# A two-layer hybrid trunk on one core: attention values in alternating column halves, recurrence products and low-rank gates over 64 rows in alternating row halves

## The chip, the cores and the metric

The kernel runs on one NeuronCore of a Trainium2 chip. A core has a matrix engine (TensorE, PE in the profile, with its weight loads listed apart as PEld), a vector engine (VectorE, DVE), an engine for activation functions (ScalarE, ACT), a general engine (GpSimd, POOL) and an engine that here only issues transfers (SyncE, SP). Matmul results land in PSUM, which the program divides into eight banks of 128 partitions by 512 float32; the other engines read them from there. Each engine works through its own instruction list strictly in the order in which the list was built, and waits at semaphores for the others.

The metric is device time in microseconds (us) of one launch. Three runs of the kernel before gave 1375.79, 1385.37 and 1380.54 us; their median, 1380.54 us, is the time to compare with.

## What is computed

The input is 1024 tokens of 1024 features. Layer 0 has two head groups beside each other, an RWKV-7 recurrence of 8 heads of width 64 and a sparse attention of 8 heads of width 64 over one shared key and value per token, of which each query keeps 256. Layer 1 is a gated linear attention. Each layer ends in an output projection and a layer norm. The parts that matter here, cut from the reference:

```python
def rwkv7_mix(r, k, v, wd, ad, w0, w2, a0, a2, ...):
    w_log = -jax.nn.softplus(-(w0 + jnp.tanh(wd) @ w2)) - 0.5     # low-rank gate, rank 64
    decay = jnp.exp(-jnp.exp(w_log))
    a = jax.nn.sigmoid(a0 + ad @ a2)                              # low-rank gate, rank 64
    ...
    def step(S, inp):
        r_t, w_t, k_t, v_t, kk_t, b_t = inp
        sa = jnp.einsum('bhvk,bhk->bhv', S, -kk_t)
        S = S * w_t[:, :, None, :] + sa[..., None] * b_t[:, :, None, :] + v_t[..., None] * k_t[:, :, None, :]
        return S, jnp.einsum('bhvk,bhk->bhv', S, r_t)

def dsa_mix(...):   # per block of 128 queries
        s = jnp.where(valid[:, :, None, :], s, -1e30)
        p = jax.nn.softmax(s, axis=-1)
        return jnp.einsum('bqhk,bqkd->bqhd', p, v_sel)

        y = jnp.concatenate([ya, yb], -1).astype(h.dtype) @ e_w_out[j]
```

## The kernel before

The kernel is one program of four stages. First come the input projections, the index scores, the RWKV operands (norms, decays, low-rank gates) and the search for the top-256 threshold; this takes about the first 515 us. From 515 to about 800 us runs the stage that most of the change is in: attention over the selected keys, with the RWKV recurrence in chunks of 64 tokens woven into it. Then follow layer 0's output projection and norm, and last layer 1.

**The order.** The program is written in Python; a scheduler then orders each engine's list by its own idea of when things are ready. Within the attention stage the Python code weaves the two parts by a credit in microseconds: `att(us)` lets the attention generator run until the credit is used, between the steps of the recurrence. The scheduler may move an instruction ahead of others on its engine where no dependence forbids it. What is finally in the list is fixed; an instruction that has to wait holds up all that stand behind it on the engine.

**Attention.** Queries go in 8 tiles of 128. For tile `i` the function `att_logits` makes the logits of all heads (L774, L775, bank `s`), and `att_out` the output: for each key tile `kt` up to `i`, it transposes the probabilities of four heads at a time (L811, bank `st`), once for the even heads (`s` = 0) and once for the odd (`s` = 1), copies them out as `pT[s]` (L813), and multiplies by the values in `values` (L795). The weights are a 128x64 tile of `v_tm`. Bank `po` holds the even heads in partitions 0 to 63 and the odd heads in 64 to 127, so that a matmul of `s` = 0 uses the array's columns 0 to 63 and one of `s` = 1 the columns 64 to 127. Each call of `values` makes four matmuls: two halves of 256 moving columns, each for both `s`. There are 36 calls in all (1 + 2 + ... + 8 key tiles), which is 144 matmuls.

**Recurrence.** The 16 chunks go in 8 units of two. For each chunk, `load_chunk` brings the operand `AT` (the chunk's a and r) into a fresh buffer: for each parity `s`, head by head, its 64 rows hold the data, and the other parity's 64 rows are set to zero by a memset on POOL (L917). `products` (L933) multiplies `BK` (the chunk's b and k of all heads, 128 rows) with `AT`: four matmuls of 128x128 by 128x128 per parity, eight per chunk, each over all 128 rows, of which 64 are zeros. Both parities use PSUM bank `g` in turn. From it ACT copies the part `MAB` (L935), and DVE writes k's products with a into `AT`'s zeroed rows (L936) and those with r into `W` (L937). `increments` (L942) transposes `BD` into bank `x`; `substitute` inverts small triangles on POOL (L964, L965), and `offdiag` finishes the inverse in four steps, all through bank `x` (L990, L999, L1009, L1018). `chain` is the serial part: per chunk Z (L1035), U (L1051), then outputs and new state (L1046, L1058), where the state's decayed part `SP` comes from POOL (L1042). `finish` transposes the normed outputs (L1102, bank `x`).

**Output projection.** When attention is over, its buffers are given to the projection's weights: 16 blocks are loaded (L124), split by ACT (`whi`, L128) and POOL (`wlo`, L129), and used by L728 to L730.

**Gates.** `decays` makes both low-rank gates for a group of heads and half the tokens: two matmuls with 64 rows each (L520), one on rows 0 to 63, the other on 64 to 127, into two banks `ix`. It is called 8 times in the first stage.

## Time and profile before

| | |
|---|---|
| runs | 1375.79, 1385.37, 1380.54 us |
| profiled execution, first to last instruction (span; its own time is given in no other form) | 1379.4 us |
| mean granted TensorE clock | 0.949 of full |
| TensorE busy | 1243.3 us, 90% |
| VectorE busy | 847.8 us, 61% |
| ScalarE busy | 564.0 us, 41% |
| GpSimd busy | 421.1 us, 31% |

A busy share is the time in which at least one instruction of the engine was under way. [...] A float32 matmul leaves two records, one for each of its two passes through the array; transposes and the matmuls of the split float32r operands leave one. Some records are missing.

### The profile page before, as it was taken

The page shows a single profiled execution, that of the slowest core. Times are in us where ns is not written, and L with a number is a line of the kernel's source. Part 1 is how long each engine was busy: PE and PEld are TensorE (multiplying, and loading weights), DVE is VectorE, ACT ScalarE, POOL GpSimd, SP SyncE. Part 2 cuts the span into 40 slices and gives each one's busy share as a digit, 9 for nine tenths or more (in the row PEclk, how much of TensorE's full clock was granted, in tenths as well). Part 3 has the DMA queues.
Part 4 walks back from the last instruction along what each step waited for, and adds up shares of the span by engine and source line. Part 5 has one row for each costly group of instructions (what it writes and reads, how often), then busy time and mean ns, then how long its engine had stood idle before and what let it go on. Part 6 is the DMA issues. An engine that isn't in the chain of part 4 may idle for free. (4 is left out here: it accounts for less than half of the span.)

```text
span 1379.4 us, 21874 instructions
## 1 busy us (share of the span) xinstructions
PE 1243.3 (90%) x8141; PEld 963.6 (70%) x8141; DVE 847.8 (61%) x2029; ACT 564.0 (41%) x1089; POOL 421.1 (31%) x532
## 2 busy tenths in 40 slices
PE   7997797887788988999999879899999999998996
PEld 6976585565566666677766658777578878887885
DVE  5345879999999456768767646683330114453665
ACT  5345757637532425555554432132551123333100
POOL 3313431341424351444444351153112221131122
PEclk9998798998899989999999989999899999999998
DMA  6102311431424378334433376561102220013131
GB/s 206 31 1 76 107 39 31 124 104 50 127 54 122 108 199 216 90 73 120 125 94 78 88 222 214 197 200 60 35 0 61 62 62 0 1 62 103 62 118 62
DMA packets 164634, 130.50 MB, mean 95 GB/s; under 512 B 61424, under 2 KB 138272, under 8 KB 164528
## 3 DMA queue, kind: packets, MB, share of 16 engines
q1 hardware_dynamic: 161728, 122.72, 30.9%
q10 hardware_dynamic: 2800, 6.39, 1.5%
q8 instruction: 64, 1.05, 0.3%
q14 instruction: 42, 0.34, 0.1%
HBM read 86.08 MB, written 42.99 MB: 94 GB/s over the span
## 5 line engine op out<-in xcount | busy, mean ns | idle before, releaser
L129 POOL TENSOR_TENSOR wlo<-wraw,whi 128x512 fp32r<-128x512 f32 (+1 forms) x80 | 100.7, 1275 | 191.2 <-ACT whi L128 126.5
L143 PE MATMUL dn<-xh,chi 128*128 128x512 f32 x336 | 137.6, 410 | 16.6 <-DVE sh L472 8.7
L145 PE MATMUL dn<-xh,clo 128*128 128x512 f32 x336 | 137.3, 409 | 0.0
L144 PE MATMUL dn<-xl,chi 128*128 128x512 f32 x336 | 136.8, 407 | 0.0
L128 ACT CAST whi<-wraw 128x512 fp32r<-128x512 f32 (+1 forms) x80 | 48.6, 613 | 130.9 <-PE dn L144 65.6
L143 PEld LDWEIGHTS dn<-xh,chi 128*128 128x128 f32 x336 | 65.8, 196 | 36.3 <-issue 11.3
L744 POOL TENSOR_TENSOR z<-z,ln 128x1024 f32<-128x1024 f32 x16 | 38.7, 2419 | 166.6 <-DVE z L743 83.2
L144 PEld LDWEIGHTS dn<-xl,chi 128*128 128x128 f32 x336 | 65.9, 196 | 20.9 <-issue 7.4
L145 PEld LDWEIGHTS dn<-xh,clo 128*128 128x128 f32 x336 | 65.8, 196 | 18.6 <-issue 5.0
L153 POOL CAST chi<-craw 128x1024 fp32r<-128x1024 f32 x21 | 25.8, 1231 | 133.3 <-PE dn L144 95.3
L380 DVE SCALAR_TENSOR_TENSOR sc<-rl,wi_s,sc 128x384 f32<-128x384 f32 (+5 forms) x42 | 50.6, 1205 | 24.4 <-ACT rl L375 22.4
L728 PE MATMUL s<-whi,yh 128*128 128x512 f32 x128 | 52.6, 412 | 14.0 <-DVE gny L118 7.1
L795 PE MATMUL po<-pT,v_tm 128*64 128x256 f32 x288 | 62.7, 400 | 0.0
L785 ACT ACTIVATE p<-p,am 128x128 f32<-128x128 f32 (+7 forms) x64 | 49.1, 769 | 18.6 <-DVE am L783 18.1
L154 POOL TENSOR_TENSOR clo<-craw,chi 128x1024 fp32r<-128x1024 f32 x21 | 54.5, 2595 | 0.9
L776 DVE CUSTOM_DVE_ANT_0 p<-s,bias_s 128x512 f32<-128x512 f32 (+1 forms) x80 | 45.4, 591 | 14.8 <-PE s L775 11.9
L729 PE MATMUL s<-wlo,yh 128*128 128x512 f32 x128 | 52.2, 408 | 0.3 <-POOL wlo L129 0.3
L641 DVE TENSOR_SCALAR_CACHE_REDUCE junk<-klo,Lc 128x384 bf16<-128x384 int16 (+1 forms) x64 | 51.8, 809 | 0.6
L641 DVE TENSOR_SCALAR_CACHE_REDUCE junk<-khi,Hc 128x384 bf16<-128x384 int16 (+1 forms) x64 | 51.8, 809 | 0.5
L1354 POOL TENSOR_TENSOR vg<-vg,sg 128x512 f32<-128x512 f32 x16 | 20.5, 1285 | 103.2 <-DVE vg L1399 66.8
L165 PE MATMUL gt<-whi,hh 128*128 128x512 f32 x128 | 51.9, 406 | 0.0
L730 PE MATMUL s<-whi,yl 128*128 128x512 f32 x128 | 51.5, 402 | 0.0
(470 smaller groups left out, 3429.1 us busy)
## 6 DMA issues: line engine op xcount, KB each, us to landing
wraw<-in_o_w_in_dram SPq DMA_DIRECT2D x48, 256.0 KB
craw<-in_e_w_in_dram SPq DMA_DIRECT2D x21, 512.0 KB
xt<-in_x_dram SPq DMA_DIRECT2D x8, 512.0 KB
d_q<-qiT SPq DMA_DIRECT2D x8, 512.0 KB
d_ar<-ar SPq DMA_DIRECT2D x8, 512.0 KB
d_gate<-sg SPq DMA_DIRECT2D x8, 512.0 KB
qT<-d_q SPq DMA_DIRECT2D x8, 512.0 KB
BK<-d_bk SPq DMA_DIRECT2D x8, 512.0 KB
```

The lines of the kernel that those rows point to most:

```text
L129: sub.tensor_sub(lo, raw, f32(hi))
L143: PE.matmul(pst, wh[:, cs], ah[:, k, sl], start=(k == 0), stop=False)
L144: PE.matmul(pst, wh[:, cs], al[:, k, sl], start=False, stop=False)
L145: PE.matmul(pst, wl[:, cs], ah[:, k, sl], start=False, stop=(k == NK - 1))
L154: G.tensor_sub(lo, raw, f32(hi))
L165: PE.matmul(pst, ah[:, k, sl], wh, start=(k == 0), stop=False)
L380: E.scalar_tensor_tensor(acc[:, a:b], r, w, acc[:, a:b], op0=ALU.mult, op1=ALU.add)
L641: V.tensor_scalar(junk[:, :n], x, c[:, z:z + 1], None, op0=ALU.is_ge, op1=ALU.add, accum_out=cnt[:, z:z + 1])
L728: PE.matmul(pt, yh[:, k, :], wh, start=(k == 0), stop=False)
L729: PE.matmul(pt, yh[:, k, :], wl, start=False, stop=False)
L730: PE.matmul(pt, yl[:, k, :], wh, start=False, stop=(k == NK - 1))
L795: inorder(PE.matmul(po[RS[s], c:c + PVN], v_tm[:, kt, :], pT[s][:, c:c + PVN], start=(kt == 0 and c == 0), stop=(kt == i), skip_group_chec ...
```

## The change

Three groups of matmuls are rewritten, with a helper `after` that gives the scheduler an order to keep between two instructions (no semaphore, and other instructions may still come between).

1. `values`: for each half of the columns now `s` = 1 first, then `s` = 0, and all four matmuls are chained in this order.
2. `products`: each matmul takes only its parity's 64 rows of `BK` and `AT`. The two parities alternate, chained, and go into two PSUM banks, `g` and `x`. The zeroed rows are no longer read here. `AT` becomes six fixed buffers in turn instead of a pool; only the r half of the zero rows, which `chain` still reads, is cleared, once per buffer ahead of the loop, and the memset per chunk and parity goes.
3. `decays`: the two gate matmuls are issued before either activation, chained.

All other differences are dropped comments and docstrings.

```diff
+    def after(prev, ins):
+        if prev is not None:
+            tc.add_manual_dep(ins.ins, prev.ins.name, mybir.DependencyInfo(
+                mybir.DependencyClass.NoSync, mybir.DependencyReason.DATA), reason="side by side")
+        return ins
...
     def decays(j, h, pool):
-        for th, row, bc in ((thw, 0, HW0), (tha, CH, HA0)):
-            pt = ptile("ix")
-            PE.matmul(pt, w2a2[row:row + CH, j * P:(j + 1) * P], wa[row:row + CH, sl], start=True, stop=True)
+        pts, last = [ptile("ix"), ptile("ix")], None
+        for pt, row in zip(pts, (0, CH)):
+            last = after(last, PE.matmul(pt, w2a2[row:row + CH, j * P:(j + 1) * P], wa[row:row + CH, sl],
+                                         start=True, stop=True))
+        for th, pt, bc in zip((thw, tha), pts, (HW0, HA0)):
             A.activation(th, pt, AF.Tanh, scale=0.5, bias=drv[:, bc + j:bc + j + 1])
...
         def values(kt, pT):
+            last = None
             for c in range(0, 512, PVN):
-                for s in range(2):
-                    inorder(PE.matmul(po[RS[s], c:c + PVN], v_tm[:, kt, :], pT[s][:, c:c + PVN],
-                                      start=(kt == 0 and c == 0), stop=(kt == i), skip_group_check=True))
+                for s in (1, 0):
+                    last = after(last, PE.matmul(po[RS[s], c:c + PVN], v_tm[:, kt, :], pT[s][:, c:c + PVN],
+                                                 start=(kt == 0 and c == 0), stop=(kt == i), skip_group_check=True))
...
+    ATB = []
+    for z in range(6):
+        ATB.append(rt([P, 4, 2, P], f"AT{z}"))
+        for s in range(2):
+            G.memset(ATB[z][RS[1 - s], :, s, CH:], 0.0)
+
     def load_chunk(u, cc):
-        S = rt([P, 4, 2, P], "AT", 6)
+        S = ATB[c % 6]
         for s in range(2):
-            G.memset(S[RS[1 - s], :, s, :], 0.0)
             nc.sync.dma_start(S[RS[s], :, s, :], d_ar[RS[s], :, c, :])
...
     def products(u, cc):
+        pts, last = [ptile("g"), ptile("x")], None
+        for j in range(4):
+            for s in range(2):
+                last = after(last, PE.matmul(pts[s][:, j * P:(j + 1) * P], BK[RS[s], j * 2 + cc, :], AT[RS[s], j, s, :],
+                                             start=True, stop=True))
         for s in range(2):
             b_, k2_ = RS[s], RS[1 - s]
-            pt = ptile("g")
-            for j in range(4):
-                inorder(PE.matmul(pt[:, j * P:(j + 1) * P], BK[:, j * 2 + cc, :], AT[:, j, s, :], start=True, stop=True))
-            p3 = pt.rearrange("p (j t) -> p j t", t=P)
+            p3 = pts[s].rearrange("p (j t) -> p j t", t=P)
             A.copy(MABv[b_, :, cc, :], p3[b_, :, 0:CH])
```

Since the scheduler orders the lists anew, the places that matter are shown as they stand in the two programs. A row has the line of the kernel, the operation, its output and inputs, the output's shape and how many follow each other. The lines of the changed kernel lie 9 to 19 higher. The first place is on TensorE, one key tile of attention; `po` is the values' bank, `st` the transposes' and `s` the logits'. Before:

```order
L811 MATMUL st<-ident,p 128x128 x4
L795 MATMUL po<-pT,v_tm 64x256
L774 MATMUL s<-KH_93,qT 128x512
L775 MATMUL s<-KL,qT 128x512
L774 MATMUL s<-KH_93,qT 128x128
L775 MATMUL s<-KL,qT 128x128
L811 MATMUL st<-ident,p 128x128 x4
L795 MATMUL po<-pT,v_tm 64x256 x3
```

The same work in the changed program:

```order
L822 MATMUL st<-ident,p 128x128 x4
L784 MATMUL s<-KH_93,qT 128x512
L785 MATMUL s<-KL,qT 128x512
L784 MATMUL s<-KH_93,qT 128x128
L785 MATMUL s<-KL,qT 128x128
L822 MATMUL st<-ident,p 128x128 x4
L806 MATMUL po<-pT,v_tm 64x256 x4
```

Before, one matmul of `s` = 0 stood alone and three (`s` = 1, 0, 1) stood together, at all 36 key tiles (at one of them the three are split further); now four stand together, at 34 of the 36, and two and two at the other two.

The second place is on TensorE too, the products of one chunk (`g` and `x` written from `BK`). Before:

```order
L1035 MATMUL zu<-RUV,AT 64x64 x8
L942 MATMUL x<-ident,BD 128x128
L933 MATMUL g<-AT,BK 128x128 x4
L1046 MATMUL sy<-RUV,AT 64x64 x8
L942 MATMUL x<-ident,BD 128x128 x3
L811 MATMUL st<-ident,p 128x128 x4
```

And in the changed program:

```order
L949 MATMUL g<-AT_3793,BK 128x128
L1077 MATMUL sy<-RUV,W 64x64 x9
L961 MATMUL x<-ident,BD 128x128 x4
L1077 MATMUL sy<-RUV,W 64x64 x7
L822 MATMUL st<-ident,p 128x128 x4
L784 MATMUL s<-KH_93,qT 128x512
L785 MATMUL s<-KL,qT 128x512
L784 MATMUL s<-KH_93,qT 128x256
L785 MATMUL s<-KL,qT 128x256
L949 MATMUL x<-AT_3793,BK 128x128
L949 MATMUL g<-AT_3793,BK 128x128
L949 MATMUL x<-AT_3793,BK 128x128
```

Before, each parity's four products stood together, in 32 groups of four. Now the first product of `g` stands alone and, after other work, the remaining seven alternate between `x` and `g`; it is so at all 16 chunks.

The third place is on POOL at the end of the stage, where the last decayed states `SP` and the split of the projection's weights (`wlo`) meet. Before:

```order
L965 TENSOR_TENSOR Xt<-Xt,itmp 128x8
L1042 TENSOR_TENSOR SP<-RUV,PC 64x256 x2
L972 TENSOR_TENSOR TT<-td,own 128x512
L1042 TENSOR_TENSOR SP<-RUV,PC 64x256 x2
L129 TENSOR_TENSOR wlo<-wraw,whi 128x512 x16
```

And in the changed program:

```order
L984 TENSOR_TENSOR Xt<-Xt,itmp 128x8
L136 TENSOR_TENSOR wlo<-wraw,whi 128x512 x2
L991 TENSOR_TENSOR TT<-td,own 128x512
L136 TENSOR_TENSOR wlo<-wraw,whi 128x512 x2
L1061 TENSOR_TENSOR SP<-RUV,PC 64x256 x2
L136 TENSOR_TENSOR wlo<-wraw,whi 128x512 x12
L1061 TENSOR_TENSOR SP<-RUV,PC 64x256 x2
```

Attention now ends two chunks earlier in the recurrence, so that the last two `SP` stand among the weights' splits and no longer ahead of them. On TensorE, 95 matmuls of the projection now stand ahead of the last chunk's first one (L1054), where none stood before. The two gate matmuls keep their places: in both programs the same 8 to 24 rows of other work stand between the two of a call.

## The prediction, made before the changed kernel ran

> **What bounds the kernel now.** I first asked which engine fills the stage of the change: the table by stretches, here attention with the recurrence (515 to 781 us), its tail until the projection's weights are in (781 to 819), and what follows. After the bounds of the stretch come busy time and instructions of PE, PEld, DVE, ACT and POOL, then the granted clock.
>
> ```profile
> 515.00:781.00 266.00, 248.84 (x3739) 186.97 (x3738) 190.68 (x566) 141.37 (x341) 111.84 (x316) 0.98 0.45 110
> 781.00:819.00 38.00, 24.06 (x247) 17.93 (x246) 19.37 (x41) 18.19 (x36) 20.10 (x16) 0.82 0.74 215
> 819.00:1000.00 181.00, 170.82 (x718) 128.21 (x719) 99.55 (x206) 52.98 (x79) 44.44 (x28) 0.95 0.44 142
> ```
>
> In the first stretch TensorE is idle for 17.2 us of 266, and VectorE, next, is busy for 72%. TensorE bounds this stage, at full clock, so that work taken off it there should shorten the run. In the tail it is idle for 13.9 us of 38. Next, its waits in the stage (us in total, times, longest):
>
> ```profile
> PE x L990 <- DVE Tn L985: 6.3, 4, 2.5
> PE x L942 <- DMA BD<-d_bd: 3.0, 1, 3.0
> PE g L933 <- issue: 1.4, 1, 1.4
> ...
> PE g L933 <- POOL AT L917: 0.3, 1, 0.3
> ```
>
> None repeats often; no single releaser sets the pace. Last, what a matmul really costs: the timeline of one key tile (start, duration until the last of a group ends, records), with two close-ups of the run of six records.
>
> ```profile
> 563.22 0.65 PE L795 MATMUL po<-pT,v_tm 128*64 128x256 f32 x2
> 563.80 0.50 PE L774 MATMUL s<-KH,qT 128*128 128x512 f32 x1
> ...
> 564.89 0.27 PE L811 MATMUL st<-ident,p 128*128 128x128 f32 x1
> 565.10 1.08 PE L795 MATMUL po<-pT,v_tm 128*64 128x256 f32 x6
> 566.10 0.50 PE L774 MATMUL s<-KH,qT 128*128 128x512 f32 x1
> ...
> 565.10 0.44 PE L795 MATMUL po<-pT,v_tm 128*64 128x256 f32 x2
> ...
> 565.58 0.38 PE L795 MATMUL po<-pT,v_tm 128*64 128x256 f32 x1
> ...
> 565.79 0.38 PE L795 MATMUL po<-pT,v_tm 128*64 128x256 f32 x1
> ```
>
> Two records at 565.10 are over within 0.44 us: the first passes of two matmuls in different column halves run side by side. The pair has its two passes done by 565.58. The third matmul then has the array alone: its passes start at 565.58 and 565.79, 0.21 apart. So a pair costs what one matmul costs. A change between array shapes (128x128, 128x64, 32x32) adds about 0.15: 0.10 of emptying before the start (564.89 plus a pass of 0.11 is 565.00, the next starts at 565.10) and 0.05 in the first pass (565.10 to 565.58 is 0.48, where two later passes take 0.43).
>
> **The change part by part.**
>
> *Values.* The lone matmul of each key tile joins the three and rides beside the one that had no partner. 36 key tiles save two passes of 0.215 each, 0.43: 15.5 us, all on the path while TensorE is the bound.
>
> [...]
>
> ```profile
> 565.09 0.20 PEld L795 LDWEIGHTS po<-pT,v_tm 128*64 128x64 f32 x4 [0.17 <-issue]
> ...
> L795 PEld LDWEIGHTS po<-pT,v_tm x288: 132/136/227, 515.4 to 780.8; 128*64 128x64 f32 x144
> ```
>
> *Products.* A group of four costs eight passes one after the other, of 0.108 each: 128 columns, half of the 256 that took 0.215. The last starts at 640.83, and with one more pass and a change of shape the next instruction at 641.04.
>
> ```profile
> 639.95 1.16 PE L933 MATMUL g<-AT,BK 128*128 128x128 f32 x8
> ...
> 640.83 0.28 PE L933 MATMUL g<-AT,BK 128*128 128x128 f32 x1
> 641.04 0.28 PE L1051 MATMUL zu<-Zs,TT 128*64 128x64 f32 x2
> ...
> 641.53 0.37 ACT L935 COPY MAB<-g 64x256 f32<-64x256 f32 x1
> ...
> 643.99 0.41 DVE L936 TENSOR_TENSOR AT<-g,GM 64x256 f32<-64x256 f32 x1
> 644.33 0.40 DVE L937 TENSOR_TENSOR W<-g,GM 128x256 f32<-128x256 f32 x1
> ```
>
> A chunk now has 16 passes (two groups). With 64 rows each the parities use different row halves. If these run side by side as the column halves do, the lone product costs two passes and the seven cost as much as the four of one row half, eight: 10 in place of 16. That saves 6 x 0.108 x 16 chunks = 10.4 us. The trace shows no matmuls in two row halves with the same columns, so that this has ends: 0, if they follow each other, and 10.4. I take 10.4, since the nearest rows, the pair in column halves above and the 32x32 products below (46 records within 0.58 us, each in another row and column quarter than the one before), both overlap. [...]
>
> ```profile
> 775.36 0.58 PE L990 MATMUL x<-Tn,MAB 32*32 32x16 f32 x46
> ```
>
> *Changes of shape.* 64x128 is a shape of its own, next to none of its neighbours. Counted over both orders from the first values to the last recurrence product, without the projection's matmuls, there are 271 changes before and 251 now: the values' merged groups save more than the split products add. 20 x 0.15 = 3.0 us less.
>
> *Gates.* One gate matmul has two passes of 512 columns, 0.43 each (twice the values' 0.215; with a change of shape, the 1.06 below from 238.19 to 239.25). Side by side, the two of a call would save one's 0.86, 6.9 us over 8 calls. But the order keeps them apart, row for row as before: 0, and with that nothing to gain or lose.
>
> ```profile
> 238.19 1.12 PE L520 MATMUL ix<-wa,w2a 64*128 64x512 f32 x2
> 239.25 0.50 PE L145 MATMUL dn<-xh,clo 128*128 128x512 f32 x1
> ```
>
> *Memsets.* POOL loses 32 memsets and gets 12 of half the size ahead of the loop:
>
> ```profile
> L917 POOL MEMSET AT<- x32: 517/519/522, 509.0 to 718.3; 64x512 f32 x32
> ```
>
> 16.6 us of POOL go, but POOL is busy for 111.84 of 266 us, and by the waits above the products waited for a memset for 0.3 us in all: 0. The loads of `AT` stay as many and in SP's queue; their cover, TensorE's work, is shorter by a tenth, and they come two units ahead.
>
> *New waits.* Bank `x`, used 7 times per unit (two increments, four steps of `offdiag`, one `finish`), is now used 9 times, and the seven products stand in TensorE's list until it is free; what is behind them waits too.
>
> ```profile
> 641.65 0.66 PE L942 MATMUL x<-ident,BD 128*128 128x128 f32 x4
> ...
> 642.35 0.59 ACT L943 COPY W<-x 128x512 f32<-128x512 f32 x1 [0.45 <-PE x L942]
> ```
>
> An increment holds the bank for 1.3 us (641.65 to 642.94), a product for 4.8 (639.95 to 644.73), most of it in VectorE's queue. Bounds: nothing, if the order has put the seven behind the readers' end everywhere; if nowhere, 1.3 for the seven and 3.8 (4.8 less their own 1.0) for the bank's next user, 16 x 5.1 = 82 us. Nearest are the present waits on `x`, 6.3 + 3.0 us over 56 uses, 0.17 each; at twice that for 16 more users: 5.4, I take +6 us.
>
> *Tail.* TensorE's longest wait stands here, with both banks `s` full behind a slow norm on VectorE:
>
> ```profile
> 811.03 0.39 PE L729 MATMUL s<-wlo,yh 128*128 128x512 f32 x1
> 811.26 0.39 PE L730 MATMUL s<-whi,yl 128*128 128x512 f32 x1
> 818.79 0.76 PE L728 MATMUL s<-whi,yh 128*128 128x512 f32 x1 [7.15 <-DVE gny L118]
> ...
> 789.52 1.26 POOL L129 TENSOR_TENSOR wlo<-wraw,whi 128x512 fp32r<-128x512 f32 x1 [13.09 <-ACT whi L128]
> ...
> 816.36 1.26 POOL L129 TENSOR_TENSOR wlo<-wraw,whi 128x512 fp32r<-128x512 f32 x1 [0.47 <-ACT whi L128]
> ```
>
> Attention now ends two chunks earlier in the recurrence, so that the weights come while TensorE still has these chunks to do. That may take away the 7.15. Against it, the last `SP` stand behind 16 splits, which took 28 us here (789.52 to 817.62); the last chunk cannot begin before, but 95 projection matmuls (0.23 apart, 811.03 to 811.26: 22 us) fill most of it, leaving up to 6. Between -7 and +6 I take -1.5, hardly a gain.
>
> Sum: -15.5 - 10.4 - 3.0 + 6 - 1.5 = -24.4 us. Against the profiled execution, a span of 1379.4, that is 1355.0; the median of the runs lies 1.1 above this span, so I predict 1356 us.
>
> **The rivals.**
>
> *Row halves do not overlap.* Without the 10.4 us: 1366.5, on the edge of 1%. For it: no row shows them. Against: every other pair of disjoint parts does.
>
> *The readers become the bound.* VectorE needs 190.68 us for this stage, and each `pT`, logit and product must be copied out before TensorE goes on. If their waits stand in series with TensorE's work, VectorE keeps its 72%, the stage its 266 us, and only the tail's 1.5 is left: 1379. Against: from 650 to 700 us VectorE was at 77% (38.67 of 50), at which the stage would take 246.6, 19 us less. Where less attention is left, chunks follow each other faster, 9.6 us (766.73 to 776.36) against 17.2 in the middle, so that the recurrence's own readers are not yet the limit:
>
> ```profile
> 650.00:700.00 50.00, 48.61 (x816) 36.57 (x814) 38.67 (x112) 27.80 (x63) 18.81 (x51) 1.00 0.47 117
> ...
> 662.37 0.69 PE L1035 MATMUL zu<-RUV,AT 128*64 128x64 f32 x16
> 679.58 0.33 PE L1035 MATMUL zu<-RUV,AT 128*64 128x64 f32 x2
> ...
> 766.73 0.69 PE L1035 MATMUL zu<-RUV,AT 128*64 128x64 f32 x16
> 776.36 0.40 PE L1035 MATMUL zu<-RUV,AT 128*64 128x64 f32 x4
> ```
>
> [...]
>
> *Bank `x` stops TensorE: slower.* With the 82 us of waits from above against 28.9 saved, 1380.5 + 82 - 28.9 - 1.5 = 1432; with half of them 1391. It decides from 28.9 / 16 = 1.8 us per chunk on, and makes the kernel slower by 1% from (28.9 + 1.5 + 13.8) / 16 = 2.8. Against: the present 0.17 per use, and an order with other work between the lone product and the seven.
>
> **How the numbers follow.** The forecast has 0.62, row halves apart 0.15, readers 0.12, bank `x` 0.11. A measurement of this kernel tells about 1% (13.8 us) from no change. Faster than 1366.7 are the forecast and half of the row halves' case: 0.69; within 1% the other half and the readers' case: 0.20, rounded; slower the bank: 0.11. The range goes from 1340 (no new waits, the 7.15 gone, and a few of the idle 17.2 us with it) to 1380, past the readers' case; bank `x` and the forecast's far end stay out. 1340 to 1368 is the forecast's own.
>
> **What would show it.** Right: values in groups of eight records, 0.91 us from first start to the last's end of pass, and about 1.0 to the next matmul; product records of 64 rows starting in twos at one time, 0.9 to 1.0 us for the seven; the stage's TensorE work 29 us shorter, the projection's first matmul about 30 us earlier. The halves' rival shows in product starts 0.108 apart throughout; the readers' in waits of `st` and `s` for DVE and ACT; the bank's in waits of the products or of L942 and L990's successors for L936 and L937. The forecast would be wrong if the merged values did not run in pairs, or if the splits held up the last chunk beyond the projection's work.

## The result and the profile after

The changed kernel takes 1396.35 us (median of 4 runs, 1393.80 to 1400.34), the kernel before in the same comparison 1380.80. The ratio is 1.0108, with a 95% interval from 1.0071 to 1.0145: slower by about 15 us, where 24 us less were forecast. The profiled execution took 1393.8 us, its span is 1392.1.

The table by stretches of the changed kernel, for the bounds that the prediction used (busy time and instructions of PE, PEld, DVE, ACT and POOL, granted clock, DMA share, GB/s):

```profile
515.00:781.00 266.00, 231.47 (x3464) 170.84 (x3464) 181.99 (x541) 133.68 (x320) 96.55 (x285) 0.91 0.43 107
781.00:819.00 38.00, 23.64 (x369) 17.86 (x370) 12.99 (x23) 19.27 (x40) 25.15 (x21) 0.70 0.74 222
819.00:1000.00 181.00, 166.44 (x824) 125.07 (x823) 96.56 (x233) 43.63 (x79) 45.76 (x28) 0.98 0.44 142
```

TensorE was busy for 248.84 of the first 266 us before and is busy for 231.47 now: the difference is idle time, and the granted clock fell from 0.98 to 0.91 (in the tail from 0.82 to 0.70). VectorE is at 68%, so that no other engine has become full. The bounds are those of the kernel before and cut the changed kernel's work elsewhere, so they don't tell how long the stage is. Its ends do: the last matmul of the values starts at 768.6 us instead of 781.0, the projection's first at 788.8 instead of 794.7 (the prediction looked for some 30 us), its last at 906.3 instead of 908.6. The waits of TensorE in attention, the recurrence and their tail (515 to 850 us; total, times, longest):

```profile
PE g L949 <- DMA BK<-d_bk: 6.6, 4, 2.7
PE x L1037 <- ACT Gs L1031: 6.4, 4, 4.2
PE s L737 <- ACT yh L1158: 6.2, 2, 3.7
PE st L822 <- ACT pT L824: 5.7, 6, 2.2
PE sy L1077 <- ACT RUV L1072: 4.6, 1, 4.6
PE x L1028 <- DVE Tn L1024: 4.3, 3, 1.9
...
PE x L1009 <- DVE Tn L1004: 0.7, 1, 0.7
```

Many waits for many releasers: one load (of `BK`, ahead of the lone product of `g`), copies on ScalarE, a transpose on VectorE. The last row is the wait that led before (L990, 6.3 us in four times); here it is all but gone.

The timeline of the changed kernel shows that the instructions themselves do what was expected. First a key tile's values with the next instruction, then seven products of 64 rows in two banks (first three and last three rows of the run; start, duration until the last of a group ends, records):

```profile
559.84 1.08 PE L806 MATMUL po<-pT,v_tm 128*64 128x256 f32 x8
560.86 0.50 PE L784 MATMUL s<-KH,qT 128*128 128x512 f32 x1
...
619.82 0.37 PE L949 MATMUL x<-AT,BK 64*128 64x128 f32 x1
619.83 0.37 PE L949 MATMUL g<-AT,BK 64*128 64x128 f32 x1
620.04 0.27 PE L949 MATMUL x<-AT,BK 64*128 64x128 f32 x1
...
620.48 0.27 PE L949 MATMUL x<-AT,BK 64*128 64x128 f32 x1
620.49 0.27 PE L949 MATMUL g<-AT,BK 64*128 64x128 f32 x1
620.60 0.38 PE L949 MATMUL x<-AT,BK 64*128 64x128 f32 x2
```

All four matmuls of a tile (eight records) are through after 1.02 us. This is read from start to start, since TensorE's records overlap: in the kernel before, the values' passes at 565.58 and 565.79 start 0.21 us apart and last 0.38 each. The products start in twos, in different row halves, 0.11 us from one pair of passes to the next: row halves do run side by side.

And the timeline at the end of layer 0. Kernel before: the recurrence's last stores and the loads of `z` for the layer norm (SyncE's queue), then the first and the last transposes of `z`:

```profile
832.43 2.59 SPq L1112 DMA_DIRECT2D d_y<-yf  x4
837.55 0.92 SPq L1244 DMA_DIRECT2D z<-d_h  x2
...
858.00 0.60 PE L175 MATMUL st<-ident,z 128*128 128x128 f32 x4
...
941.69 0.60 PE L175 MATMUL po<-ident,z 128*128 128x128 f32 x4
```

The same in the changed kernel:

```profile
865.73 2.55 SPq L1131 DMA_DIRECT2D d_y<-yf  x4
869.96 0.80 SPq L1263 DMA_DIRECT2D z<-d_h  x2
...
889.31 0.60 PE L182 MATMUL st<-ident,z 128*128 128x128 f32 x4
...
967.67 0.60 PE L182 MATMUL po<-ident,z 128*128 128x128 f32 x4
```

In both the loads for the norms start 2 to 3 us behind the recurrence's last store (so in all runs below but e4, where it is 9.5), and eight norms take about 100 us. The recurrence ends 33 us later than before, and the norms end 26 us later.

Where the recurrence falls behind shows in the first products of its chunks (Z, `zu`). The 13th chunk and the 16th, the last, before:

```profile
754.96 0.69 PE L1035 MATMUL zu<-RUV,AT 128*64 128x64 f32 x16
...
792.02 1.57 PE L1035 MATMUL zu<-RUV,AT 128*64 128x64 f32 x16 [3.62 <-DVE RUV L1066]
```

And in the changed kernel:

```profile
766.67 0.70 PE L1054 MATMUL zu<-RUV,AT 128*64 128x64 f32 x16
...
835.23 0.69 PE L1054 MATMUL zu<-RUV,AT 128*64 128x64 f32 x16
```

Twelve us are lost up to the 13th chunk, and 31 more from there to the 16th: each of these three steps takes 22 to 23 us where they took 10 to 16 before. They are the ones that now stand among the weights' splits and the projection's matmuls.

**An account for all runs.** From TensorE's records and the clock's marks in the trace I worked out, from 515 us to the projection's last matmul: the work (busy time, with what falls into marks of half clock counted half: a key tile's values take 1.91 us there, from 610.20 to 612.11 in the changed kernel, against 1.02 at full clock), what half clock added to it, and idle time; further the starts of the projection's last matmul, of the recurrence's last store and of the last transpose of `z`, and the span of the profiled execution. All in us; the names are those of the runs below. Each row is one execution, and one kernel's executions lie up to 17 us apart (those of e2, e4, e5, e7, e11 and e14 were the slowest of their kernel's, those of the changed kernel, e3, e6 and e12 the fastest), so that a few us between two rows mean little and the medians decide.

```
run                      work  half clock  idle   proj. end  last store  last z   span
before                  344.4     12.5     36.8     908.6      834.4     942.0   1379.4
after                   316.5     26.0     48.9     906.3      867.7     968.0   1392.1
e1_values               328.8     20.4     46.0     910.1      852.0     958.2   1386.4
e2_products             337.9     24.1     38.3     915.3      877.8     972.5   1398.8
e3_incr_g               317.1     23.1     51.5     906.6      840.4     945.1   1381.1
e4_splits_late          319.2     38.5     69.8     942.5      848.4     968.4   1413.2
e5_values_old_order     324.4     23.2     44.6     907.2      833.4     939.4   1376.6
e6_old_values_new_order 328.9     22.5     43.1     909.4      850.0     955.3   1381.2
e7_before_other_weave   345.3     13.7     32.0     906.0      848.9     951.0   1375.2
e8_filled_gaps          351.5     11.4     26.4     904.2      833.5     936.7   1372.5
e9_more_value_work      363.2      7.3     29.6     915.1      844.9     948.2   1384.0
e10_other_weave_values  325.5     16.5     40.2     897.2      840.4     941.8   1367.4
e11_after_bk_twice      318.4     30.6     49.0     913.0      874.4     974.2   1397.9
e12_after_short_norm    317.3     23.3     51.6     907.2      868.5     953.5   1377.4
e13_before_short_norm   343.4     17.6     29.3     905.3      839.0     934.1   1371.5
e14_both_and_filled     343.7     12.5     29.3     900.5      843.7     945.3   1371.2
e15_after_more_value_wk 333.6     24.4     45.7     918.8      880.1     977.4   1401.1
```

Two things can be read off before any experiment. First, the work fell by 27.9 us, as forecast (28.9), but 13.5 us came back as half clock and 12.1 as idle time, so that the projection ended only 2.3 us sooner. Second, the end of layer 0 hangs on two chains. The last matmul of layer 1's first values comes at the later of "projection's end + 52.9" and "last transposes of `z` + 7.5": 961.5 by the first in the kernel before (seen: 961.5), 975.5 by the second in the changed kernel (seen: 975.1). The two offsets are taken from the traces, not derived. The rule fits the other runs to 1.5 us, except e3 and e13 (4 to 5 us), and what comes after takes 416 to 420 us in each. So the account of the loss in the trace (12.7 us of span) is -2.3 us by the projection, and then +16 because the other chain took over.

### The profile page after: what moved, and what is told of

Its sections match the earlier page's. It is cut to its first block, busy times and chain, and to the rows that moved or that the text cites. A ratio compares the mean times of both kernels' runs of the same rounds, so it can differ in the third digit from the quotient of the medians.

```text
span 1392.1 us, 21824 instructions
## 1 busy us (share of the span) xinstructions
PE 1234.2 (89%) x8141; PEld 953.2 (68%) x8141; DVE 840.0 (60%) x2029; ACT 563.2 (40%) x1089; POOL 411.8 (30%) x512
## 4 chain that ended last, share of the span: by engine, by line
PE 45%; DVE 24%; DMA 9%; issue 8%; ACT 6%; POOL 5%; SPq 1%; POOLq 0%; DVEq 0%; ACTq 0%
DVE junk L650 6%; PE dn L152 3%; PE dn L150 3%; PE dn L151 3%; PE op L737 2%; PE op L738 2%; PE op L739 2%; PE gt L172 2%; PE gt L173 2%; PE gt L174 2%; DVE sc L387 2%; DMA z<-d_h 2%; PE po L806 1%; PE ix L173 1%; PE ix L174 1%
## 5 line engine op out<-in xcount | busy, mean ns | idle before, releaser
L822 PE MATMUL st<-ident,p 128*128 128x128 f32 x288 | 52.1, 303 | 8.5 <-ACT pT L824 5.7
L983 POOL TENSOR_TENSOR itmp<-Mt,Xt 128x30 f32<-128x30 f32 (+10 forms) x120 | 30.7, 256 | 70.3 <-DMA Mt<-d_m 62.1
```

The lines of the kernel that those rows point to most:

```text
L822: inorder(PE.transpose(pt[:, j * P:(j + 1) * P], ps[2 * j + s][:, kt * P:(kt + 1) * P], ident))
```

## The experiments

Ratios are to the kernel before, measured beside each run, with 95% intervals; its median there lay between 1378.43 and 1382.12 us, so compare ratios and not microseconds. The first four runs were made under the theory that the loss lies in the tail alone (weights' splits and casts among the last chunks), against the theories that bank `x` or TensorE's waits in the stage cause it.

**e1: the values alone.** Only `values` has the new form; products and gates are those of before.

```diff
-                for s in range(2):
-                    inorder(PE.matmul(po[RS[s], c:c + PVN], ...
+                for s in (1, 0):
+                    last = after(last, PE.matmul(po[RS[s], c:c + PVN], ...
```

> Only the values alternate; products, their banks and AT as before. In its order 16 Z matmuls of the recurrence stand behind the last value (8 before, 24 in the changed kernel), and all 16 weight splits stay behind the last SP. Tail theory (the loss comes from the splits' place among the recurrence's last chunks): the values' 15 us come, 1364 to 1374. Rival (merging the values itself starves the recurrence): 1385 or more. Value groups of four should cost about 1.0 us in both.

Measured: 1390.12 us, ratio 1.0059 [1.0031, 1.0086]. Slower, with the tail's new banks and products gone. TensorE's work fell by 15.6 us, and half clock (+7.9) and idle time (+9.2) took it all. The tail theory in its first form falls.

**e2: the products alone** (and the fixed `AT` buffers).

```diff
+        pts, last = [ptile("g"), ptile("x")], None
+        for j in range(4):
+            for s in range(2):
+                last = after(last, PE.matmul(pts[s][:, j * P:(j + 1) * P], BK[RS[s], ...], AT[RS[s], ...], ...
```

> Only products over 64 rows in two banks, with the fixed AT buffers; values as before. 24 Z matmuls stand behind the last value and the splits among the last SP, as in the changed kernel. Tail theory: 1395 to 1415, the changed kernel without the values' gain. Rival (the products gain and the values lose): 1365 to 1378.

Measured: 1393.23 us, ratio 1.0072 [1.0048, 1.0096]. The recurrence's last store is even later than in the changed kernel (877.8). So each part alone makes the kernel slower. Their sum would be 1.3% against the 1.1% of both together, which the intervals do not tell apart.

**e3: the increments' transposes in bank `g`**, otherwise the changed kernel without the gates' part (in the traces every engine does the first 500 us, where the gates are, in the same order with and without it).

```diff
     def increments(u, cc):
-        pt = ptile("x")
+        pt = ptile("g")
```

> Values and products as changed, but the increments' transposes go to bank g, which the products have half left, instead of x. Its order has 16 Z matmuls behind the last value and all splits behind the last SP. Bank theory (x was crowded, and with it the scheduler put the recurrence late): 1358 to 1370, TensorE's waits from 515 us to the last value under 25 us. Rival (64-row products or the clock themselves cost the time, wherever they stand): 1388 to 1400.

Measured: 1386.98 us, ratio 1.0040 [1.0017, 1.0062]. Faster than the changed kernel by 9 us, but TensorE's work, half clock and idle time are nearly the same as there (317.1, 23.1, 51.5). What differs is the new list that this edit drew as well: the recurrence's last store comes 27 us sooner. It tells little of bank `x`.

**e4: the casts of the projection's weights behind the recurrence's copies.** Like e3 the changed kernel without the gates' part; ScalarE's casts stand in its list behind chunk 14's copy of `RUV`, and the projection's buffers are opened after the recurrence has been written out.

```diff
-            A.copy(hi, raw)
+            after(behind, A.copy(hi, raw))
...
-            A.copy(R[RS[1], :, 1, :], Uv[RS[1]])
+            hold[c] = A.copy(R[RS[1], :, 1, :], Uv[RS[1]])
...
         if ep is None:
-            open_pieces()
+            return
```

> Values and products as changed, with bank x as changed; only the casts of the projection's weights on ScalarE are ordered behind the recurrence's copy of U in chunk 14. The stage up to the last value stays as in the changed kernel. Tail theory: the recurrence's last product at 810 to 825 instead of 848, and 1372 to 1384. Bank theory (the loss is made before the last value): 1390 to 1400.

Measured: 1408.99 us, ratio 1.0191 [1.0145, 1.0236]. The recurrence ended 19 us sooner than in the changed kernel, the projection 36 us later. The two chains of the end trade against each other: here, getting one out of the way by delaying the other lost.

After these four, every part that touches the code near attention had made the kernel slower, whatever it did. Each had also drawn all five lists anew. From here on lists were pinned: at the end of the program the instructions of each engine are chained in a given order (a dependency that only keeps the order).

**e5: the values' work in the old lists.** The lists are those of before, entry by entry; only the lone matmul of each key tile moves in front of its three. (The code is shortened; `ORDER` is a packed list of instruction numbers, and its change is told below in words.)

```diff
+    traced = {i.name: i for i in nc.cur_bb.bb.instructions}
+    for names in ORDER:
+        for prev, name in zip(names, names[1:]):
+            tc.add_manual_dep(traced[name], prev, mybir.DependencyInfo(
+                mybir.DependencyClass.NoSync, mybir.DependencyReason.DATA), reason="order")
...
 ORDER, TensorE, each key tile:
-  ..., s0c0, ..., s1c0, s0c1, s1c1, ...
+  ..., s0c0, s1c0, s0c1, s1c1, ...
```

> Only the values are changed, and each engine's list is pinned to that of before, entry by entry (a chain over the whole list); the one thing that moves is the lone matmul of each key tile, put directly in front of its three. Less TensorE work as in the values-only run, without its new list. Theory A (the new list is what costs: its waits and the half clock behind them ate the work saved): the 15.5 us come through, 1362 to 1371 us, the values' cost near 41 us, TensorE's waits in 515 to 781 as in before. Rival B (the stage is bound by its readers and loads, whatever the list): no gain, 1377 to 1384, with the saved time back as waits of st, s or g. Rival C (less work on TensorE lowers the granted clock by itself): 1385 to 1395, the stage's waits little longer but the time at half clock in 515 to 900 up from 31 us to 45 or more.

Measured: 1373.34 us, ratio 0.9966 [0.9951, 0.9982]: faster than before, by 4.7 us. Against e1, which does the same work in its own lists, it is 0.93% or 12.8 us faster, more than both intervals leave room for. So the lists are a cause of their own (theory A). But only 5 us came of 20 us less work. In the account the rest came back as half clock (+10.7) and idle time (+7.8). The waits of TensorE in the stage show where most of the idle time arose:

```profile
PE x L990 <- DVE Tn L985: 12.3, 4, 6.0
PE x L942 <- DMA BD<-d_bd: 2.8, 2, 2.5
PE st L811 <- DVE pT L813: 2.1, 5, 1.0
```

Before, the first of them was 6.3. The timeline of one such place, unit 2. Kernel before (the chunk's copied product on ScalarE, the last matmul ahead of the wait, the matmul that waited):

```profile
591.04 0.37 ACT L935 COPY MAB<-g 64x256 f32<-64x256 f32 x1 [0.23 <-PE g L933]
...
618.58 0.65 PE L795 MATMUL po<-pT,v_tm 128*64 128x256 f32 x2
621.71 1.05 PE L990 MATMUL x<-Tn,MAB 32*32 32x16 f32 x64 [2.49 <-DVE Tn L985]
```

And in e5:

```profile
589.37 0.37 ACT L935 COPY MAB<-g 64x256 f32<-64x256 f32 x1
...
614.74 0.66 PE L811 MATMUL st<-ident,p 128*128 128x128 f32 x4
621.44 0.77 PE L990 MATMUL x<-Tn,MAB 32*32 32x16 f32 x41 [6.04 <-DVE Tn L985]
```

TensorE arrives 3.8 us sooner and starts only 0.3 sooner. Between the copy and this matmul lie 30.3 us before and 31.7 now: masking on POOL, a sum, a store and a load, 15 steps on POOL, another store and load, masking again, a transpose on VectorE. No matmul stands in this chain, so that fewer matmuls don't make it shorter. It began 1.7 us sooner, with the copy, and lost 1.4 of them again on its way (single steps on POOL and the second store took longer); why is not known.

**e6: meant to put the old work into e1's lists.** The lists of e1, but a tile's four matmuls in the order s = 1, 1, 0, 0.

```diff
-            for c in range(0, 512, PVN):
-                for s in (1, 0):
+            for s in (1, 0):
+                for c in range(0, 512, PVN):
```

> The other corner: each engine's list pinned to that of the values-only run, but a tile's four matmuls go s = 1, 1, 0, 0, so that only the middle two can ride together: TensorE's work as in before (three times 0.43 us a tile in place of two). Theory A: the list alone makes it slower than before, by the values-only run's 9 us plus most of the 15.5 us put back: 1396 to 1406 us. Rival B: the work put back falls into waits that are there anyway: 1388 to 1392, as the values-only run (1390). Rival C: more work keeps the clock up, so that it is faster than the values-only run: 1380 to 1388.

Measured: 1385.92 us, ratio 1.0065 [1.0045, 1.0084], as e1. But the premise was wrong: the work did not come back (328.9 against e1's 328.8). The timeline of a tile, and the starts of its first four records in the trace:

```profile
560.03 1.09 PE L802 MATMUL po<-pT,v_tm 128*64 128x256 f32 x8
561.05 0.33 PE L780 MATMUL s<-KH,qT 128*128 128x128 f32 x1
```

```
560.032  560.045  560.299  560.312
```

Two matmuls of one column half stand ahead of two of the other, and still both halves start within 13 ns. The strict alternation does nothing here; that the four stand together does all of it. As a test of the lists the run is only a repeat of e1. As such it shows no cost of pinning: 1.0065 with the lists pinned, 1.0059 without. (The records don't name their half. That those 13 ns apart are of different halves follows from two passes in one half being 0.215 apart; in e1, where the partner is the next in the list, they are 7 ns apart.)

**e7: the old work in other lists.** The kernel before with one number of the planner changed, from 2.2 to 2.3.

```diff
-ATT, ATT1, ATT2, FC = (2.2, 1.2, 1, 10)
+ATT, ATT1, ATT2, FC = (2.3, 1.2, 1, 10)
```

> The kernel before with one number of its planner changed, the cost put down for one burst of attention, 2.2 to 2.3: the same instructions and operands, another list (two chunks instead of one are left when attention ends). Theory A: a list drawn anew costs by itself, 1386 to 1400 us. Rivals B and C: the same work takes the same time, 1377 to 1385.

Measured: 1373.16 us, ratio 0.9964 [0.9944, 0.9983]. The same instructions in another order are 5 us faster. Theory A's guess, that a list drawn anew costs, was wrong in its sign: it may go either way, between -5 us here and +13 in e1 against e5.

**e8: TensorE's gaps filled.** e5 with 107 matmuls of the identity in seven places with gaps of 2.5 to 7.2 us.

```diff
+    def warm(pt, n):
+        for _ in range(n):
+            PE.matmul(pt[:, 0:P], ident, ident, start=True, stop=True)
```

> The run of the values in the old list (1373 us), every list the same, and in TensorE's list 107 idle-time matmuls added (identity times identity, 128x128 by 128 columns, 0.22 us each, overwritten by the matmuls behind them or read by nobody), in seven places where that run's trace has a gap of 2.5 to 7.2 us and, after it, TensorE at half clock: ahead of the increments of unit 1 (9), the first products of the substitution of units 2, 5 and 6 (20, 10, 11), the last chunk's first products (15), and the third and twelfth piece of the projection (28, 14). Theory D (the half clock follows the gaps and costs half of the 46 us that TensorE works at it): time at half clock in 515 to 910 falls from about 58 us to under 25, and the run takes 1358 to 1368 us. Rival E (the half clock has another cause, or what it slows lies beside waits anyway): half clock as before, or less of it with the same end, 1371 to 1377; by 23 us of added matmuls on the path up to 1396 where the gaps do not come again.

Measured: 1374.19 us, ratio 0.9935 [0.9911, 0.9959]. At unit 2 the wait is gone and the first product starts when it did in before and in e5:

```profile
616.38 4.63 PE L764 MATMUL x<-ident 128*128 128x128 f32 x40
621.40 0.73 PE L996 MATMUL x<-Tn,MAB 32*32 32x16 f32 x64 [0.39 <-DVE Tn L990]
```

What half clock added fell from 23.2 to 11.4 us, and the mean granted clock of all executions is 0.948 to 0.955 against 0.939 to 0.946 in e5: the half clock follows the gaps. But the run gained only 0.3% over e5, and the intervals touch. Theory D had the mechanism right and its price too high. The likely reason is that much of what half clock slows runs into a wait anyway; it was not measured by itself.

**e9: more work of the values, in the old lists.** The lone matmul of each tile is issued twice.

> The other direction: the lists of before, and directly behind the lone matmul of each of the 36 key tiles the same matmul once more (that part of the values is counted twice in the output), 0.43 us each, 15.5 us of TensorE work more. If TensorE bounds the stage, as the prediction said, it costs what it takes: 1392 to 1398 us. If waits and the tail decide (as the 5 us for 19 us less of work say), it costs little: 1379 to 1386. In between, a knee: work added costs nearly in full, work taken away gives a quarter.

Measured: 1385.94 us, ratio 1.0031 [1.0014, 1.0048]. 15.5 us of matmuls by forecast (18.8 by the account) cost 4.3 us. The wait at the substitution, 12.3 us in e5 and 6.3 before, shrinks, as the waits of e9 show:

```profile
PE x L993 <- DVE Tn L988: 1.5, 2, 1.0
```

No knee: work added and work taken away both count for a quarter to three tenths; in the traces half clock and idle time move against it (12.5 and 36.8 before, 7.3 and 29.6 here, 23.2 and 44.6 in e5).

**e10: the values' work in e7's lists**, with the lone matmul moved as in e5.

> The merged values, as in the run with the old list, but in the list of the run with the other planner number (1373 us; attention ends one chunk earlier), each list pinned to it. If the worth of the merged values hangs on the list only through the waits, again some 5 us: 1366 to 1371. If the two small gains are one and the same slack: 1371 to 1376. If TensorE bounds the stage in this list: 1358.

Measured: 1373.73 us, ratio 0.9930 [0.9902, 0.9957]. That is 0.34% below e7, which was measured at another time, the same step as in e5, though here the intervals overlap.

**e11: `BK` in two buffers**, in the changed kernel's own lists.

```diff
-        BK, BD = rt([P, 8, P], "BK"), rt([P, 8, P], "BD")
+        BK, BD = rt([P, 8, P], "BK", 2), rt([P, 8, P], "BD")
...
-        Mt = rt([P, HB, HB], "Mt", 2)
+        Mt = rt([P, HB, HB], "Mt")
```

> The changed kernel with its own lists pinned, and BK in two buffers in place of one (Mt in one in place of two, for the room). It takes away the longest of its waits in the stage, the lone product of g behind the load of BK (6.6 us in four waits), and nothing else. If the stage's waits decide: 1386 to 1391, by the 6.6 us and some of the half clock behind them. If the end hangs on the recurrence's last store, through the norms behind it: by what that store comes earlier, 1388 to 1394; and if neither, 1394 to 1398 as the changed kernel itself (1396).

Measured: 1397.88 us, ratio 1.0113 [1.0084, 1.0142], as the changed kernel. The wait went only from 6.6 to 4.5 us:

```profile
PE st L822 <- ACT pT L824: 8.2, 6, 4.9
PE x L1037 <- ACT Gs L1031: 6.6, 4, 4.5
PE g L949 <- DMA BK<-d_bk: 4.5, 4, 1.5
```

So most of it is not the buffer (the load's place in SyncE's queue is the likely rest, which was not tried). What was gained there may be lost at `st`, which now leads, or to `Mt`, which lost its second buffer; the run does not tell.

**e12 and e13: a shorter norm, in the changed kernel and in the kernel before.** Lists pinned, layer 0's norm without scale and shift.

```diff
-        V.tensor_mul(z, z, gb[0])
-        G.tensor_add(z, z, gb[1])
+        if scaled:
+            V.tensor_mul(z, z, gb[0])
+            G.tensor_add(z, z, gb[1])
```

> The changed kernel with its lists pinned, and the norm of layer 0 without its scale and shift (left out of the output): 8 passes of VectorE (1.2 us) and 8 of GpSimd (2.4 us) less, all in the chain load z, norm, transpose that starts when the recurrence's last store is out. Two-chain theory: the changed kernel's end hangs on that chain (its last transposes of z at 968.0 us, layer 1's values 7 us behind them), and the other chain, the projection's last matmul plus 53 us, would allow 959. The chain gets some 3.6 us per tile shorter, so that the other one takes over: 12 to 16 us faster than the changed kernel, 1380 to 1385 us. Rival (the norm lies beside other work, and TensorE's idle time from 900 to 1000 has another cause): 1391 to 1396.

> The same cut in the kernel before, its lists pinned. Two-chain theory: there the projection's end decides (908.6 + 52.9), and the norms' chain has 12 us to spare, so that little comes of it: 1376 to 1381 us, at most 3 us less than before. Rival: as much as in the changed kernel.

Measured: 1385.36 us, ratio 1.0036 [1.0016, 1.0057], for the changed kernel, 10 us less than it takes uncut; 1373.17 us, ratio 0.9944 [0.9925, 0.9963], for the kernel before, 7.7 us less. The traces go as the two chains have it. In the changed kernel the recurrence's last store and the projection's end stay where they were, the last `z` comes 14.5 us sooner, and the span is 14.7 us shorter:

```profile
870.83 0.80 SPq L1264 DMA_DIRECT2D z<-d_h  x2
...
953.21 0.60 PE L182 MATMUL po<-ident,z 128*128 128x128 f32 x4
```

In the kernel before, the projection itself ended 3.3 us sooner and layer 1's values another 4.6, presumably because the passes left out also stood in the way of the projection's readers. That is more than the 3 us allowed for, and in the medians the two cuts cannot be told apart (0.72 against 0.56%, each uncertain by 0.2 to 0.4). The chain of the norms is thus supported by the traces of all runs, and not settled by this pair.

**e14: both and filled.** e10 with 76 matmuls of the identity in seven gaps.

> What the runs point to, put together: the merged values in the list of the other planner number, and 76 idle-time matmuls (identity, 0.22 us) where that run's trace shows gaps of 2.1 to 5.4 us: ahead of the increments of unit 1 (11), the first products of the substitution of units 2, 5 and 6 (18, 8, 11), the second products of chunk 14 (12), and the first and the last piece of the projection (7, 9). If the half clock's cost is partly real, as the run with filled gaps says (4 us for 7 filled places): 1364 to 1372 us. If that was chance: 1370 to 1377 as without.

Measured: 1369.43 us, ratio 0.9919 [0.9898, 0.9940]. The fastest kernel of the study, 0.8% ahead of the kernel before; that the filling helps over e10 is not shown.

**e15: the values' work put back into the changed kernel's lists.** At each tile the first of the four is issued twice.

```diff
+                    if s == 1 and c == 0:
+                        PE.matmul(po[RS[s], c:c + PVN], v_tm[:, kt, :], pT[s][:, c:c + PVN], ...
```

> The changed kernel with its lists pinned, and at each of the 36 key tiles the first of the four matmuls (s = 1, first half of the columns) once more directly behind itself, so that a tile's values take three times 0.43 us as in the kernel before, not two (that part is counted twice in the output). 15.5 us of TensorE work come back, the list stays. If the stage gives a quarter to a third for work added or taken away, as in the list of before: 4 to 6 us slower than the changed kernel, 1399 to 1403 us, and the list alone then stands for the whole loss and more. If the merged values had been worth their 15.5 us: 1409 to 1413. If they cost by themselves (less work, more half clock): 1390 to 1396.

Measured: 1401.84 us, ratio 1.0143 [1.0093, 1.0193]. The added work does run serially in its column half: the tile below takes 1.43 us, from 567.45 to the next instruction at 568.88, where the changed kernel's four matmuls take 1.02 (L809 is the added one):

```profile
567.45 0.66 PE L806 MATMUL po<-pT,v_tm 128*64 128x256 f32 x4
567.93 0.38 PE L809 MATMUL po<-pT,v_tm 128*64 128x256 f32 x1
567.94 0.42 PE L806 MATMUL po<-pT,v_tm 128*64 128x256 f32 x1
```

It costs 0.35%, 4.8 us, again some three tenths, though by itself this difference is inside the intervals. With the values' work as before, the changed kernel's lists (with the new products and their banks in them) are 1.4% slower than those of before, although the products still take less.

## Why the prediction was wrong

**The work was right.** By the account the values fell from 51.0 to 35.5 us, 15.5 as forecast. The products fell from 31.4 to 23.9, 7.5 in place of 10.4; the row halves overlap, but a pair takes 0.11 us per pass, and the lone product and its change of shape take 0.4 each, where two passes, 0.22, were put down. All else fell by 4.9, where 3.0 were forecast for the changes of shape; that the sum comes within 1 us of the forecast (27.9 against 28.9) is in part luck. The gates' term was 0 and is: in the traces every engine does the first 500 us in the same order with and without that part.

**The step that failed first** is the one ahead of the sum: "TensorE bounds this stage, at full clock, so that work taken off it there should shorten the run". It read 94% of busy time and the absence of a leading wait as a bound. Four changes of the values' work inside fixed lists (e5, e9, e10 against e7, e15 against the changed kernel) moved the time by 4.3 to 4.8 us for the forecast's 15.5. e5 and e9 are shown by their intervals, the other two agree with them. At the size of e5 the term of -15.5 was worth -4.7. In the old lists (e5) the substitution's chain of 30 us through POOL, VectorE and DMA is what TensorE came to wait for in unit 2, and work taken off ahead of it became idle time. The prediction quoted that very wait, 6.3 us in four times, and used it only to price bank `x`. In the changed kernel's own lists that chain is not the limit: TensorE waits 0.7 us for its transpose and, in units 1 to 6, reaches the product that reads it 8 to 16 us after the transpose starts. Its waits are spread over many releasers, and why work counts for so little there too (e15) stays open.

**The new lists had no term.** The prediction counted positions in them (shapes, the lone matmul, the splits) but took the weave as neutral. With the same values, e1's lists cost 12.8 us against e5's. The planner's small number moved the kernel before by -5 us. With the values' work put back, the changed kernel is 1.4% behind before. That outweighs what the saved work brought.

**The tail, -1.5 with bounds of -7 and +6, was mis-sized.** It asked whether TensorE had other work while the last chunks waited for the splits, and it had: the projection ended 2.3 us sooner. But that work went ahead of the chunks: from the 13th to the 16th they took 69 us instead of 37. And it didn't ask who waits for the recurrence's end. The norms of layer 0 do; the last store is 33 us later, and the second chain, which had 12 us to spare before (949.5 against 961.5), now ends 16 us behind the first. In the trace this is the whole loss. With the norms made shorter the changed kernel gains 10 us in the medians (e12); but the kernel before gained too (e13), so that the share of this chain in the medians is not shown.

**New waits on bank `x`, +6.** The seven products hardly wait (0.5 us in all ahead of those into `x`). The place that waits is the lone product of `g`, 6.6 us for `BK`, which the prediction had not named. Taking a part of that wait away gave nothing (e11); in that trace other waits had grown. Neither that nor e3 settles what the bank costs beyond the list that comes with it.

**The rivals.** "The readers become the bound", at 1379 us, was nearest for the values alone (e5: 0.9966, that is 1376 of 1380.8), but for another reason: not VectorE's throughput, which stays at 68% in the changed kernel, but, in the old lists, the latency of a chain: in the trace of e5 TensorE's waits for the substitution's transpose come to 12.3 us, those for the copies out of `st` on VectorE and ScalarE to 2.1 and 1.8. The rival with a slower result named bank `x`; the traces show no wait on it that would explain the loss, but its share in the lists that came with it is not shown.

What stays open is which places of the changed kernel's lists make the recurrence late: of the 43 us by which the last chunk starts later, the trace puts 31 behind the 13th chunk, but no run moved the projection's matmuls out of there with all else kept. It was not tried to pin the new products into the old lists, since they need bank `x` at other times.

## What to carry to other kernels

An engine that is busy for 94% of a stage is not thereby its bound: look whether a chain on other engines meets it at fixed points, and measure the slope by adding a known dose of work before counting on savings. Where a planner draws the lists anew for every edit, time the edit in pinned old lists too, since the new weave alone may be worth as much as the edit, with either sign. And for the end of a stage, ask of each chain that leaves it who starts when it ends, not only which engine has work in the meantime.

## What the runs showed of the hardware

- Column halves pair without alternation: in e6 the order 1, 1, 0, 0 starts both halves 13 ns apart and takes 1.02 us for the four, as 1, 0, 1, 0 does in the changed kernel. A matmul of one half starts 13 ns behind one that stands two places ahead of it in the list, and so ahead of the one between them: on TensorE starts don't keep the order of the list strictly.
- Row halves (64 rows, 128 columns, float32, different banks) run in pairs of passes 0.11 us apart in the changed kernel, as close as single passes of 128 rows in the kernel before (0.108).
- The clock's marks show half clock in stretches, from 515 to 905 us six of 3.4 or 6.8 us in the kernel before and ten of 3.4, 6.8, 10.2 or 20.5 us in the changed kernel, mostly behind gaps in TensorE's work. In all 17 traces from 515 to 905 us, a window of 3.4 us at half clock stands behind one in which TensorE was idle for 1.8 us in the median, a window at full clock behind one with 0.0. In e8, filling seven gaps halved what this cost (23.2 to 11.4 us), yet the time changed by 0.3% in the medians, with intervals that overlap.
